# The product with w_out by seven quarter products, its weight sums split early and kept in DRAM

## The chip, the cores and the metric

The kernel runs on one core of a Trainium2 chip. The metric is the time of one execution on the device in microseconds (us), the median of three runs. A difference of 0.2% is 2.4 us here.

The engines are named as in the profile: PE multiplies matrices (PEld is its weight load), DVE, ACT and POOL work elementwise, SP issues the DMAs between DRAM and the on-chip memory. Each runs its own instructions in order.

## The reference

It is one block of a streaming encoder, for 1024 tokens of width 1024 and 16 meta tokens ahead of them. What matters here:

```python
z = einsum('bld,dn->bln', rmsnorm(h), w_in)          # a, q, k, v, r, lr, ga, gb
p = pool_mix(multiscale_pool(a)) * pool_scale        # four groups of 128 channels
y_a = p @ w_pool_out
y_b = (rmsnorm(gla(q, k, v, log_a)) * silu(r)) @ w_gla_out
m = sigmoid(ga) * y_a + sigmoid(gb) * y_b
h = h + m @ w_out                                    # the product that is changed
h = h + square(relu(rmsnorm(h) @ w_ff1)) @ w_ff2
return rmsnorm(h)[:, N_META:]
```

## The kernel before

**Products.** All is float32. A factor is kept as two fp32r parts, high and low (`w1h`, `w1l`; `th`, `tl`), and `mm3` (L281 to L287) multiplies by three matmuls: high by high (L285), and the two mixed ones (L286, L287). One matmul is 128x128 by 128x512 at most. To split a factor, ACT copies its high part and DVE subtracts that for the low part. PE runs its matmuls in the order of the program text; for DVE, ACT, POOL and SP a scheduler sets an order when the kernel is built.

**The stage of the a-blocks** (60 to 150 us). After the value projections come four blocks `a_block(g)` (PE, 72 matmuls of two 264-column pieces and one of 512 columns for each of the three parts), the decays, and `mix_block(g)`: DVE makes the trailing sums `s` of group g (L665, one to four instructions of 128 x 1024 or a little more), subtracts the token (L668), ACT and DVE split the outcome into `ph` (L671, L672), and PE multiplies it by a 128x128 matrix, six matmuls to the banks `b_mm` and `b_sc`. The list in the text is a0, decays 0, a1, decays 1, mix 0, a2, mix 1, a3, mix 2, k0, mix 3; then come `differences`, which takes the differences of the input's quarters (`xr`) and splits them to `t0`, `t1`, `t2` (ACT L704, DVE L705), and k1. The weights of each block are loaded by SP to two buffers `raw`. From 150 us on POOL makes sums of weights for the later products (`fs`, `s`, L810).

**The merge stage** (480 to 590 us). The blocks `yb(j)` for the second half of the tokens multiply by w_gla_out, and DVE joins the outcome with `gb` and `ma`, which SP loads from DRAM to lent buffers `o` and `t` (L1137, L1195, L1196); the outcome is split to `MH`, `ML`. `load_wo` loads w_out in 256-row pieces by 512 columns and splits it in place. `out_tile(t, ch)` is the product with w_out for 128 tokens and 512 output columns: 8 contraction blocks of 3 matmuls, in all 8 x 2 x 24 = 384 matmuls of 128x512. Its outcome is added to the input x in `acc`, followed by the layer norm, a store of h, and `turn_tile`, which transposes the rows for the feed-forward product and makes the quarter differences for it. Three `mm` banks and three `ms` banks are there.

Of the kernel before, what the change touches and what calls it, by code (L numbers as in the profile page):

```python
# [7 lines left out]
F32 = mybir.dt.float32  # L8
# [6 lines left out]
P = 128  # L15
# [107 lines left out]
def kernel(  # L123
# [55 lines left out]
    h_dram = dp.tile([8, P, D], F32, name="h_dram")  # L179
    hf_dram = [dp.tile([NPAIR, P, HALF], F32, name=f"hf{m}_dram") for m in range(7)]  # L180
# [425 lines left out]
    def decays(p):  # L606
        def fn():
            for half, c in enumerate(halves()):
                y = nxt("c")
                log_decay(S["lr"][:, c], p, HALF, y, nxt("t1"))  # L610
                act.activation(y, y, ACT.Exp, scale=1.0 / TAU)
                nc.sync.dma_start(decay_dram[p, half], y)
                yield 0.6
            if p:
                act.activation(gnorm, gnorm, ACT.Copy, scale=0.5)
            log_decay(S["lr"][:, SEQ : SEQ + META], p, META, metab[:, META_LOG[p]], metab[:, 4])
            if p:
                tc.keep_in_program_order(act.preload_act_table_set("exp_and_others"))

        return fn  # L620

    def pool_open():
# [4 lines left out]
        lr_turn()  # L627
        act.activation(S["gu"], wgu, ACT.Copy)
# [62 lines left out]

    def differences():

        left.pop_to(S["left_t"])
# [25 lines left out]
    for f, i in ((a_, 0), (d_, 0), (a_, 1), (d_, 1), (m_, 0), (a_, 2), (m_, 1), (a_, 3), (m_, 2), (k_, 0), (m_, 3)):  # L720
        f(i)
# [365 lines left out]
    def gla_open():  # L1087
        left.pop_to(S["left_t"])
        right.pop_to(0)
        S["yg"] = {h: right.push(f"yg{h}", [P, 2, HEADS, HALF], F32R) for h in (1, 0)}  # L1090
# [81 lines left out]
    def yb_block(j, h):  # L1172
        def fn(wb=None):
# [8 lines left out]
            for e in range(2):  # L1182
                d, w = 2 * j + e, slice(e * P, (e + 1) * P)
                ask()
                gl, ml = take("b", d, h)
                b = bank("mm")
# [8 lines left out]
                dve.scalar_tensor_tensor(gl, gl, 1.0, b, ALU.add, ALU.mult)  # L1195
                dve.tensor_tensor(gl, gl, ml, ALU.add)  # L1196
                th = MH[h][:, d]
                tl = ML[h][:, d]
                act.activation(th, gl, ACT.Copy, scale=0.5)
                dve.scalar_tensor_tensor(tl, gl, 0.5, f32(th), ALU.mult, ALU.subtract)  # L1200
# [111 lines left out]

    def merge_open():
        banks(keep=2, ms=3)
        left.pop_to(left_m)
        right.pop_to(1)
        S["wo"] = [left.push("wo0", [P, 2, KT, HALF], F32R)]
# [3 lines left out]
        S["left2"] = left.mark()  # L1321
        buffer("t1", 4)
        buffer("o", 4)
        lend("t1", "o")
        wanted[:] = [("b", 2 * j + e, 1) for j in MERGE for e in range(2)]
        ask()
        raw.lend(left.push("raw3", [P, D], F32))
        nc.sync.dma_start(gB, bcast(norm_ffn))

    def x_again(*rows):  # L1330
        for t in rows:
            tc.keep_in_program_order(nc.sync.dma_start(S["acc"][:, t], x[t * P : (t + 1) * P, :]))

    def load_wo(ch, kk):
        def fn():
            wo = S["wo"][ch][:, :, 2 * kk : 2 * kk + 2]
            c = slice(ch * HALF, (ch + 1) * HALF)
            src = w_out[kk * 256 : (kk + 1) * 256, c].rearrange("(k p) c -> p k c", p=P)
            if ch:
                r = raw.load(src, D).rearrange("p (k c) -> p k c", k=2)  # L1340
            else:
                r = S["acc"][:, 4 + kk].rearrange("p (k c) -> p k c", k=2)
                nc.sync.dma_start(r, src)
            act.activation(wo[:, 0], r, ACT.Copy)
            dve.tensor_tensor(wo[:, 1], r, f32(wo[:, 0]), ALU.subtract)

        return fn

    step(rest, merge_open)
    def wo1_open():  # L1350
        raw.back()
        left.pop_to(S["left2"])
        right.pop_to(0)
        S["u2p"] = right.push("u2p", [P, 2, HALF], F32)
        raw.lend(right.push("rawx0", [P, D], F32))
        S["right_ff"] = right.mark()
        S["wo"].append(right.push("wo1", [P, 2, KT, HALF], F32R))


    ORDER = (0, 4, 1, 5, 2, 3, 6, 7)  # L1360

    def out_tile(t, ch):
        def fn():
            half, at = t // 4, (t % 4) * P
            wo = S["wo"][ch]
            if ch == 0 and t < 6:
                x_again(t + 2)
            if ch == 0 and t == 6:
                act.activation(gB, gB, ACT.Copy, scale=-0.5)
            b, n = bank("mm"), ORDER.index(t)  # L1370
            for j in range(2):
                if ch and j and n > 1:
                    turn_tile(ORDER[n - 2])
# [4 lines left out]
            a = S["acc"][:, t, ch * HALF : (ch + 1) * HALF]  # L1378
            dve.tensor_tensor(a, b, a, ALU.add)
            if ch:  # L1380
                layer_norm(S["acc"][:, t], S["u2"][:, n % 2])
                nc.sync.dma_start(h_dram[t], S["acc"][:, t])

        return fn

    def turn_tile(t, tags=("ms",)):
# [3 lines left out]
        u, acc, g = S["u2"][:, ORDER.index(t) % 2], S["acc"], t % 4  # L1390
# [21 lines left out]
        dve.tensor_tensor(hi, hi, lo, ALU.subtract)  # L1412
        for n, a in enumerate((lo, b12)):
            fh, fl = (S["wo"][0][:, k, 4 * n : 4 * n + 4, cols] for k in range(2))
            act.activation(fh, a, ACT.Copy)
            dve.tensor_tensor(fl, a, f32(fh), ALU.subtract)
# [4 lines left out]
    yb(2)  # L1421
    for k in range(4):
        step(rest, load_wo(0, k))
    yb(3)
    yb(0)
    step(rest, lambda: x_again(0, 1))
    step(rest, out_tile(0, 0))
    yb(1)
    step(rest, out_tile(1, 0))
    step(rest, wo1_open)  # L1430
    for t in range(2, 8):
        step(rest, out_tile(t, 0))
        if t < 6:
            step(rest, load_wo(1, t - 2))


# [3 lines left out]
    def first_blocks():  # L1440
        raw.n = 0
        for i, u in ((0, 0), (0, 1), (1, 0)):
            load_ff(i, u)

    step(rest, first_blocks)
    for t in ORDER[:6]:
        step(rest, out_tile(t, 1))
    step(rest, lambda: ff_weights())
    for t in ORDER[6:]:
        step(rest, out_tile(t, 1))  # L1450

    def ff_weights():
# [4 lines left out]
        n = lambda j: tuple(S["wo"][0][:, k, 4 * j : 4 * j + 4] for k in range(2))  # L1457
        S["x"] = {"P1": m(0, 0), "P2": m(0, 1), "P5": m(1, 0), "P3": m(1, 1), "P6": n(0), "P7": n(1)}

    def ff_open():  # L1460

        right.pop_to(S["right_ff"])
        S["fs"] = right.push("fs", [P, 2, HALF], F32)
        S["s3"] = right.push("s3", [P, HALF], F32)
        S["u3p"] = right.push("u3p", [P, 2, HALF], F32)
        S["x"]["P4"] = tuple(right.push("t4" + k, [P, 4, HALF], F32R) for k in "hl")
        raw.lend(right.push("rawx1", [P, D], F32))
        load_ff(1, 1)

    def ff_room():  # L1470

        fh, fl = S["x"]["P4"]
# [207 lines left out]
    def ff_layers():  # L1680
# [3 lines left out]
        for n in range(4):  # L1684
            if n in (1, 3):
                turn_tile(ORDER[6 + n // 2], ("mm", "ms"))
            next(run)
# [51 lines left out]
```

## Time and profile before

| | us |
|---|---|
| median of 3 runs (lowest, highest) | 1210.67 (1210.05, 1210.98) |
| span of the profiled execution | 1209.1 |
| between that span and the median | 1.6 |
| PE busy in the span | 1194.4 (99%) |
| DVE busy | 837.5 (69%) |
| ACT busy | 574.4 (48%) |
| POOL busy | 79.1 (7%) |

The profile shows one execution; the runs' times hold besides the span what the program needs to start and to end. A page row with a line, an engine and "out<-in" stands for a group of instructions by the program's names. A row of the timeline has the start in us, the busy time in us, the engine, the line, the operation with shapes, how many instructions it stands for, and in brackets the idle time before and what ended it. In the rows of the 40 slices each digit is the busy share of 30.2 us in tenths.

### The profile page before, as it was taken

The numbers are of one execution on the slowest core, as the hardware profiler recorded it, in microseconds if no ns is written. First come the engines' busy times: TensorE is split into PE (matmuls) and PEld (weight loads), VectorE is DVE, ScalarE is ACT, GpSimd is POOL, SyncE is SP. The second block draws the span as 40 slices with busy tenths as digits, with TensorE's granted clock in tenths as the row PEclk, the third lists the DMA queues.
The fourth block names the chain that finished last, engine by engine and source line by source line (L and its number), as shares of the span: only waits on it lengthen the run. The fifth ranks groups of instructions, "written<-read, shape, count | busy, mean of one in ns | idle before, by whom it ended". The sixth has DMA issues, their size and how long they took to land.

```text
span 1209.1 us, 18303 instructions
## 1 busy us (share of the span) xinstructions
PE 1194.4 (99%) x6775; PEld 993.1 (82%) x6775; DVE 837.5 (69%) x1369; ACT 574.4 (48%) x1014; POOL 79.1 (7%) x97
## 2 busy tenths in 40 slices
PE   9999999999999999999999999999999999999997
PEld 7999877878778887788788888888888888888886
DVE  6636567565686669726887767677675887887686
ACT  7546444444456124305655545455464444444554
POOL 0000062323320000000000000000000000000000
PEclk9999999999999999999999999999999999999999
DMA  8223253534348978812255444444479963333532
GB/s 245 77 60 123 91 133 110 166 110 146 112 138 296 315 218 268 284 32 87 88 161 168 151 139 157 148 160 151 152 253 318 348 229 98 98 100 91 173 96 88
DMA packets 151385, 192.79 MB, mean 159 GB/s; under 512 B 12216, under 2 KB 86256, under 8 KB 151296
## 3 DMA queue, kind: packets, MB, share of 16 engines
q1 hardware_dynamic: 151136, 191.56, 49.5%
q8 instruction: 53, 0.87, 0.3%
q14 instruction: 36, 0.29, 0.1%
q10 hardware_dynamic: 160, 0.07, 0.0%
HBM read 128.66 MB, written 62.93 MB: 158 GB/s over the span
## 4 chain that ended last, share of the span: by engine, by line
PE 68%; DVE 3%; issue 1%; DMA 1%; ACT 1%; DVEq 0%; ACTq 0%
PE b_oa L287 5%; PE b_oa L285 5%; PE b_oa L286 5%; PE b_y L285 4%; PE b_y L286 4%; PE b_y L287 4%; PE b_mm L285 4%; PE b_mm L287 4%; PE b_mm L286 4%; PE b_ob L287 4%; PE b_ob L285 4%; PE b_ob L286 4%; PE b_z L286 3%; PE b_z L285 3%; PE b_z L287 3%; PE b_sc L285 2%
## 5 line engine op out<-in xcount | busy, mean ns | idle before, releaser
L774 ACT ACTIVATE w1h<-raw 128x512 fp32r<-128x512 f32 x106 | 65.8, 622 | 51.2 <-PE b_sc L286 21.2
L285 PE MATMUL b_sc<-th,w1h 128*128 128x512 f32 x216 | 85.4, 395 | 0.4 <-ACT u2p L1522 0.4
L285 PE MATMUL b_z<-th,w1h 128*128 128x512 f32 x216 | 84.9, 393 | 0.4 <-DVE c L893 0.4
L775 DVE TENSOR_TENSOR w1l<-raw,w1h 128x512 fp32r<-128x512 f32 x106 | 72.5, 685 | 18.0 <-ACT w1h L774 18.0
L286 PE MATMUL b_sc<-tl,w1h 128*128 128x512 f32 x216 | 84.8, 393 | 0.0
L286 PE MATMUL b_z<-tl,w1h 128*128 128x512 f32 x216 | 84.2, 390 | 0.4 <-DVE tl L1408 0.4
L287 PE MATMUL b_sc<-th,w1l 128*128 128x512 f32 x216 | 84.4, 391 | 0.0
L287 PE MATMUL b_z<-th,w1l 128*128 128x512 f32 x216 | 84.1, 389 | 0.0
L774 ACT ACTIVATE w1h<-fs 128x512 fp32r<-128x512 f32 x81 | 51.1, 630 | 67.0 <-PE b_y L286 33.6
L775 DVE TENSOR_TENSOR w1l<-fs,w1h 128x512 fp32r<-128x512 f32 x81 | 57.7, 712 | 23.7 <-ACT w1h L774 23.7
L285 PE MATMUL b_mm<-th,w1h 128*128 128x512 f32 (+1 forms) x208 | 72.0, 346 | 0.0
L287 PE MATMUL b_mm<-th,w1l 128*128 128x512 f32 (+1 forms) x208 | 71.1, 342 | 0.0
L286 PE MATMUL b_mm<-tl,w1h 128*128 128x512 f32 (+1 forms) x208 | 71.0, 342 | 0.0
L774 ACT ACTIVATE w1h<-bt 128x512 fp32r<-128x512 f32 x46 | 29.1, 632 | 70.8 <-issue 43.9
L1598 DVE TENSOR_TENSOR bt<-w,w 128x512 f32<-128x512 f32 x80 | 54.7, 683 | 2.7 <-DMA w<-in_w_ff_dram 2.7
L285 PE MATMUL b_mm<-wo,th 128*128 128x512 f32 x128 | 50.4, 394 | 0.9 <-PE b_mm L287 0.9
L287 PE MATMUL b_mm<-wo,tl 128*128 128x512 f32 x128 | 49.9, 390 | 0.0
L286 PE MATMUL b_mm<-wo,th 128*128 128x512 f32 x128 | 49.8, 389 | 0.0
L285 PE MATMUL b_y<-wo,w1h 128*128 128x512 f32 x128 | 49.8, 389 | 0.0
L286 PE MATMUL b_y<-wo,w1h 128*128 128x512 f32 x128 | 49.8, 389 | 0.0
L287 PE MATMUL b_y<-wo,w1l 128*128 128x512 f32 x128 | 49.8, 389 | 0.0
L775 DVE TENSOR_TENSOR w1l<-bt,w1h 128x512 fp32r<-128x512 f32 x46 | 31.8, 691 | 25.6 <-ACT w1h L774 25.6
(425 smaller groups left out, 3317.1 us busy)
## 6 DMA issues: line engine op xcount, KB each, us to landing
hf_dram<-h SPq DMA_DIRECT2D x112, 256.0 KB, 2.1
raw<-hf_dram SPq DMA_DIRECT2D x112, 256.0 KB, 2.6
w<-in_w_ff_dram SPq DMA_DIRECT2D x64, 256.0 KB, 4.8
raw<-in_w_in_dram SPq DMA_DIRECT2D x22, 512.0 KB, 4.7
raw<-in_w_ff_dram SPq DMA_DIRECT2D x16, 512.0 KB, 4.1
rawx<-in_w_ff_dram SPq DMA_DIRECT2D x16, 512.0 KB, 4.1
rawp<-in_w_in_dram SPq DMA_DIRECT2D x10, 512.0 KB, 4.2
xs<-in_x_dram SPq DMA_DIRECT2D x8, 512.0 KB, 4.8
```

The costliest lines, as they stand in the source:

```text
L285: pe.matmul(ps, ah, bh, start=first and i == 0, stop=False, skip_group_check=more)
L286: pe.matmul(ps, ah, bl, start=False, stop=False, skip_group_check=more)
L287: pe.matmul(ps, al, bh, start=False, stop=last and i == n - 1, skip_group_check=more)
L774: act.activation(hi, a, ACT.Copy)
L775: dve.tensor_tensor(lo, a, f32(hi), ALU.subtract)
L1598: dve.tensor_tensor(bt, w, S["w2"][q[3:]][:, i], ALU.add if q[2] == "+" else ALU.subtract)
```

## The change

The product with w_out is done by seven products of quarters (the form of Strassen's method that reuses sums) in place of the eight that its four quarters would need: `product(p, t)` for p in P1 to P7 and four token tiles of 128, each 4 contraction blocks of 3 matmuls, in all 7 x 4 x 12 = 336 matmuls of 128x512. Four of the seven weights are sums of w_out's quarters (T1 to T4).

These sums are made in the stage of the a-blocks, in four parts k of 128 rows each. A part loads four 256 KB pieces of w_out to `wr`; POOL makes four differences in two 256-column instructions each (L712 of the new file); ACT copies the high part of each to `ws` (L713); POOL subtracts it for the low part (L715), again in two instructions; SP writes high and low to the new `ws_dram` (L717). That makes 64 instructions of POOL, 16 of ACT and 48 DMAs in the four parts. `wr` holds one part, `ws` two differences. `wr` and `ws` lie at the end of the on-chip memory where `differences` later puts the top of `t2`, so it begins with `right.pop_to(3)`.

In the merge stage the second half's outcomes stay unsplit in `acc`, those of the first half are written to `mo_dram` and read again; `first_sums` and `last_sums` make the token sums on DVE, ACT and POOL; `ready` reads the finished weight sums from `ws_dram`, `staged` loads and splits the plain quarters. The blocks `yb` have four halves of `u2` as their buffers for `gb` and `ma`; two `mm`, two `x` and two `ms` banks are there. PE adds P6, P7 and P4 to banks that hold earlier products, and ACT, POOL and DVE add the banks to x in `acc`. The gates' factor 0.5 is taken into earlier scales.

```diff
+        S["wr"] = right.push("wr", [P, 4, HALF], F32)
+        S["ws"] = right.push("ws", [P, 2, 2, HALF], F32R)
...
+    def wo_load(k):
+        for j in range(4):
+            nc.sync.dma_start(S["wr"][:, j], wo_rows(j, k))
+
+    def wo_sums(k):
+
+        b11, b12, b21, b22 = (S["wr"][:, j] for j in range(4))
+        both = (slice(0, 256), slice(256, HALF))
+        for n, (to, a, b) in enumerate(((b11, b12, b11), (b12, b22, b12), (b22, b22, b11), (b21, b21, b22))):
+            hi, lo = (S["ws"][:, n % 2, u] for u in range(2))
+            for c in both:
+                pool.tensor_tensor(to[:, c], a[:, c], b[:, c], ALU.subtract)
+            act.activation(hi, to, ACT.Copy)
+            for c in both:
+                pool.tensor_tensor(lo[:, c], to[:, c], f32(hi[:, c]), ALU.subtract)
+            for u, a in enumerate((hi, lo)):
+                nc.sync.dma_start(ws_dram[(0, 2, 1, 3)[n], k, u], f32(a))
...
     def differences():
 
+        right.pop_to(3)
         left.pop_to(S["left_t"])
...
-    for f, i in ((a_, 0), (d_, 0), (a_, 1), (d_, 1), (m_, 0), (a_, 2), (m_, 1), (a_, 3), (m_, 2), (k_, 0), (m_, 3)):
+    o_ = lambda k: step(one, wo_ahead(k))
+    step(one, lambda: wo_load(0))
+    for f, i in (
+        (a_, 0), (o_, 0), (d_, 0), (a_, 1), (o_, 1), (d_, 1), (m_, 0), (a_, 2), (o_, 2), (m_, 1), (a_, 3), (o_, 3), (m_, 2),
+        (k_, 0), (m_, 3),
+    ):
...
     def merge_open():
-        banks(keep=2, ms=3)
+        banks(keep=1, mm=2, x=2, ms=2)
...
+        buffer("u2", 2, D)
+        S["io"] = [S["u2"][:, i, c] for i in range(2) for c in halves()]
...
-    def out_tile(t, ch):
...
-                mm3(
-                    b, KT // 2, lambda i: (MH[half][:, 4 * j + i, at : at + P], ML[half][:, 4 * j + i, at : at + P]),
-                    lambda i: (wo[:, 0, 4 * j + i], wo[:, 1, 4 * j + i]), first=j == 0, last=j == 1,
-                )
...
+    def product(p, t):
...
+        mm3(b, 4, lambda k: (ah[:, k, c], al[:, k, c]), lambda k: (w[:, 0, k], w[:, 1, k]), first=first, more=not first)
+        (c11, c12), (c21, c22) = ([S["acc"][:, 4 * r + t, h] for h in halves()] for r in range(2))
+        if p in ("P1", "P6", "P7"):
+            act.activation(c21, b, ACT.Copy)
+            pool_add({"P1": c11, "P6": c12, "P7": c22}[p], c21)
+            return
```

Lines of the new file are numbered anew: L665, L668, L672 and L705 of before are L670, L673, L677 and L741, and L1137 is L1179.

**DVE, from the first mix block's sums on.** The names: `s` the trailing sums of a mix block, `ph` its split factor, `metab` small values of the meta tokens, `t2l` the low part of the last difference, `xr` the input. Before, `t2l` stands ahead of all the mix blocks:

```order
L400 COPY lrtok<-b_mm 16x16
L705 TENSOR_TENSOR t2l<-xr,t2h 128x2048
L412 TENSOR_TENSOR lr<-b_ms,lr 16x16
L412 TENSOR_TENSOR lr<-b_ms,lr 16x512 x2
L85 TENSOR_TENSOR w1l<-raw_120,w1h 128x1024
L665 TENSOR_TENSOR s<-a 128x1024
L668 SCALAR_TENSOR_TENSOR s<-s,a 128x1024
```

Now it stands between the sums and the subtraction of the last mix block, g = 3 (the four L670 are that block's sums):

```order
L670 TENSOR_TENSOR s<-a 128x1038
L670 TENSOR_TENSOR s<-s 128x1036
L670 TENSOR_TENSOR s<-s 128x1032
L670 TENSOR_TENSOR s<-s 128x1024
L741 TENSOR_TENSOR t2l<-xr,t2h 128x2048
L673 SCALAR_TENSOR_TENSOR s<-s,a 128x1024
L677 TENSOR_TENSOR ph<-s,ph 128x512 x2
```

`t2l` has moved behind some forty rows, and since its memory was that of `wr` and `ws`, it has gained waits: for POOL's last instruction of the sums and for the last writes to `ws_dram`. L673 and the `ph` of mix 3 stand behind it.

**ACT, at the second mix block.** `a` is the evacuation of an a-block, `ph` the split factor of mix 1, `c` the evacuation of a mix product. Before:

```order
L677 ACTIVATE c<-b_sc,small 128x512
L652 ACTIVATE a<-b_mm 128x264 x2
L671 ACTIVATE ph<-s 128x512 x2
L84 ACTIVATE w1h<-raw_120 128x1024
L652 ACTIVATE a<-b_mm 128x512
```

Now:

```order
L657 ACTIVATE a<-b_mm 128x264
L713 ACTIVATE ws<-wr 128x512 x2
L676 ACTIVATE ph<-s 128x512 x2
L84 ACTIVATE w1h<-raw_122 128x1024
L657 ACTIVATE a<-b_mm 128x512
L713 ACTIVATE ws<-wr 128x512
```

Two copies of part 2 (of 0 to 3), each of which waits for differences that POOL makes, stand ahead of mix 1's `ph`; copies of part 1 stand in the same way ahead of mix 0's.

**SP, at the block yb(3) of the merge stage.** Before, the pairs of `gb` and `ma` follow each other with a load of w_out now and then:

```order
L1137 DMA o<-gb_dram 128x512
L1137 DMA o<-ma_dram 128x512
L1137 DMA o<-gb_dram 128x512
L1137 DMA o<-ma_dram 128x512
L1343 DMA acc<-in_w_out_dram 128x2x512
L1137 DMA t_4683<-gb_dram 128x512
```

Now four loads of x, and elsewhere four of w_out, stand between two pairs:

```order
L1398 DMA tmp<-in_w_out_dram 128x512 x2
L1243 DMA mo_dram<-o 128x512
L1388 DMA acc<-in_x_dram 128x512 x4
L1179 DMA u_4826<-gb_dram 128x512
L1179 DMA u_4826<-ma_dram 128x512
L1179 DMA u_4826<-gb_dram 128x512
L1179 DMA u_4826<-ma_dram 128x512
L1398 DMA tmp<-in_w_out_dram 128x512 x4
```

The pairs go to four buffers in place of the eight of `t` and `o`, and stand behind the loads of the staged quarters.

More of the change, by code (lines that the diff above doesn't have):

```diff
@@ L1328, in merge_open @@
+        S["tmp"] = right.push("tmp", [P, 4, HALF], F32)
+        staged("P1")
         nc.sync.dma_start(gB, bcast(norm_ffn))
[L1330 to L1347, printed above, removed]
```

248 lines of the change are left out of this document (174 added, 74 removed).

## The prediction

> **What bounds the kernel now.** The page comes first: its busy times, then its 40 slices.
>
> ```profile
> span 1209.1 us, 18303 instructions
> PE 1194.4 (99%) x6775; PEld 993.1 (82%) x6775; DVE 837.5 (69%) x1369; ACT 574.4 (48%) x1014; POOL 79.1 (7%) x97
> PE   9999999999999999999999999999999999999997
> POOL 0000062323320000000000000000000000000000
> PEclk9999999999999999999999999999999999999999
> ```
>
> PE is at work in every slice at full clock; POOL works only from the sixth slice (151 us) to the twelfth. So time is saved only by taking matmuls away, and lost wherever PE is made to wait. The waits of PE today are small, by its longest ones:
>
> ```profile
> PE b_ms L474 <- POOL xr L459: 1.5, 1, 1.5
> PE b_gs L995 <- DVE gi L1050: 1.0, 2, 0.7
> PE b_mm L285 <- DVE o L1195: 0.9, 1, 0.9
> ```
>
> (Total, times, longest.) After a start-up wait of 1.5 us none is over 1.0 us. PE's order is that of the text, so a wait on any block's operands holds back all that follows.
>
> **The matmuls that go.** In the product with w_out the timeline of PE shows
>
> ```profile
> 501.11 0.39 PE L285 MATMUL b_mm<-wo,th 128*128 128x512 f32 x1
> 502.47 0.39 PE L285 MATMUL b_mm<-wo,th 128*128 128x512 f32 x1
> ```
>
> Between these lie six matmuls: 1.36 / 6 = 0.2267 us each. 384 become 336, so 48 x 0.2267 = **10.9 us** of PE goes. That is the whole gain; DVE and ACT work that goes or comes is worth nothing by itself.
>
> **What is added early.** The sums for four of the weights are made while PE runs the a-blocks. POOL is idle there today; the price is in its groups (busy, mean ns, idle before) and in two pairs of 128x256 instructions:
>
> ```profile
> L810 POOL TENSOR_TENSOR s<-rawp,rawp 128x256 f32<-128x256 f32 x10 | 7.2, 739 | 15.3 <-DVE w1l L775 15.3
> L810 POOL TENSOR_TENSOR fs<-raw,fs 128x256 f32<-128x256 f32 x12 | 11.7, 994 | 20.3 <-DVE w1l L775 17.4 <-DVE small L1045 2.9
> 152.92 1.43 POOL L810 TENSOR_TENSOR s<-raw,raw 128x256 f32<-128x256 f32 x2
> 224.75 2.40 POOL L810 TENSOR_TENSOR fs<-fs,raw 128x256 f32<-128x256 f32 x2 [3.73 <-DVE w1l L775]
> ```
>
> The first pair took 1.43 us, 0.715 each; the second, the same work, 2.40 us. What ran beside the second on DVE:
>
> ```profile
> 224.59 0.83 DVE L1019 TENSOR_TENSOR f<-gi,g 128x512 f32<-128x512 f32 x1
> 225.32 1.22 DVE L1030 TENSOR_TENSOR n<-n,g 128x512 f32<-128x512 f32 x1
> L1030 DVE TENSOR_TENSOR n<-n,g x4: 679/702/1220, 169.9 to 337.1; 128x512 f32<-128x512 f32 x4
> ```
>
> The DVE instruction took 1.22 us against 0.68 at best (minimum, median, maximum stand in the last row): from 225.32 it waited for POOL's first, then POOL's second waited for it. Both read two operands from on-chip memory. So POOL loses about one DVE instruction's length whenever such a one runs beside it.
>
> Now the chain of the four parts. SP issues part 0's loads just ahead of a weight load; the costs of the transfers are on the page (us to landing).
>
> ```profile
> 71.32 17.13 SPq L118 DMA_DIRECT2D raw<-in_w_in_dram  x2
> 472.63 0.45 SPq L1137 DMA_DIRECT2D o<-gb_dram  x1
> hf_dram<-h SPq DMA_DIRECT2D x112, 256.0 KB, 2.1
> raw<-hf_dram SPq DMA_DIRECT2D x112, 256.0 KB, 2.6
> w<-in_w_ff_dram SPq DMA_DIRECT2D x64, 256.0 KB, 4.8
> ```
>
> First loads landed: 71.3 + 2.6 = 73.9. Four parts of 16 POOL instructions: 4 x 16 x 0.715 = 45.8 us. Between two parts the next part's second load waits on SP behind the last write of this one: 2 x 0.45 + 2.6 = 3.5 us, three times 10.5. So POOL ends at 130.2 us if nothing hinders it. DVE has this to do until then:
>
> ```profile
> core 0: us, PE busy (x) PEld busy (x) DVE busy (x) ACT busy (x) POOL busy (x), PEclk, DMA share, GB/s
> 100.00:137.00 37.00, 37.00 (x230) 33.53 (x229) 25.42 (x33) 20.83 (x39) 0.00 (x0) 1.00 0.39 121
> 75.16 2.29 DVE L705 TENSOR_TENSOR t2l<-xr,t2h 128x2048 fp32r<-128x2048 f32 x1 [1.78 <-ACT t2h L704]
> 127.15 3.76 DVE L665 TENSOR_TENSOR s<-s 128x1036 f32<-128x1036 f32 x3
> 130.95 1.22 DVE L668 SCALAR_TENSOR_TENSOR s<-s,a 128x1024 f32<-128x1024 f32 x1
> 132.93 1.29 DVE L672 TENSOR_TENSOR ph<-s,ph 128x512 fp32r<-128x512 f32 x2 [0.76 <-ACT ph L671]
> 134.14 0.17 DVE L966 TENSOR_TENSOR metab<-metab 128x16 f32<-128x16 f32 x1
> 135.26 2.29 DVE L705 TENSOR_TENSOR t0l<-xr,t0h 128x2048 fp32r<-128x2048 f32 x1 [0.95 <-ACT t0h L704]
> 136.36 0.39 PE L285 MATMUL b_mm<-ph,mw 128*128 128x512 f32 x1
> ```
>
> Of 25.4 us DVE busy from 100 to 137, some 4.4 belong to 130.95 and after (1.22 + 1.29 + 0.17 + the 1.74 of a 2.29 us split that begins at 135.26); 21.0 us run before, nearly all with both operands on chip. POOL is at work in 45.8 / 56.3 = 0.81 of its chain, so 0.81 x 21.0 = **17.0 us** is what it loses. The bounds are 0 (DVE falls into POOL's gaps, or doesn't hinder it) and 21.0 plus some 3 for what runs from 74 to 100, so 24. I take 17, since the two pairs above show a full exchange turn by turn. POOL ends at 147.2.
>
> **Who waits for POOL.** In the new order `t2l`, which ran at 75.16, stands on DVE between the sums and the subtraction of mix 3, and it waits for POOL's last instruction and the last write. Behind it stand L668's successor, the `ph` of mix 3 and all that DVE does later. So: POOL's end + issue and landing 0.45 + 2.1 + `t2l` 2.29 = +4.8; then from L668's start to the first `ph` pair's end, 130.95 to 132.93 + 0.65, 2.6 us. Mix 3's second matmul, which reads the low `ph`, can run at POOL's end + 7.4; PE wants it at 136.36 + 0.23 = 136.6. Unhindered: 130.2 + 7.4 - 136.6 = 1.0 us lost. With 17.0 us of hindrance: **18.0 us**; at the upper bound 25. Today the same `ph` is ready at 133.6, 3.0 us ahead of PE. That cover is gone, and PE has nothing else to run.
>
> The ACT copies that wait for POOL stand ahead of mix 0's and mix 1's `ph` too; what PE waits there counts within the 18, since it shifts PE's wish for mix 3 by as much. Nothing makes this good later: the products after mix 3 need DVE and PE alike, and PE is at full load.
>
> That PE sits idle for many us in one piece is not seen in this trace. [...]
>
> The other early edits cost nothing. 48 transfers of 256 KB, 12 MB, are added where the DMA share is 0.39 in the windows row above. The weight loads of the later blocks wait on SP behind the writes that POOL releases; PE is late by as much, so they stay ahead of it.
>
> **The merge stage.** It is the other place of PE's small waits.
>
> ```profile
> 480.00:500.00 20.00, 18.33 (x80) 14.89 (x81) 15.71 (x24) 5.66 (x8) 0.00 (x0) 1.00 0.93 314
> 520.00:540.00 20.00, 20.00 (x90) 16.57 (x89) 3.98 (x6) 0.96 (x2) 0.00 (x0) 1.00 0.00 1
> 480.80 0.50 PE L285 MATMUL b_mm<-yg,w1h 128*128 128x512 f32 x1 [0.90 <-DVE o L1195]
> 490.12 0.47 PE L285 MATMUL b_mm<-wo,th 128*128 128x512 f32 x1 [0.87 <-PE b_mm L287]
> 482.26 0.69 DVE L1195 SCALAR_TENSOR_TENSOR t<-t,b_mm 128x512 f32<-128x512 f32 x1 [1.51 <-DMA t<-gb_dram]
> ```
>
> Around 480 to 500 us the DMAs are 0.93 busy, DVE waits for `gb` and PE for DVE. From 520 to 540 DVE is busy 3.98 of 20 us and the DMAs are idle: the new token sums (28 DVE instructions of 0.69) and the reads of the finished weights (32 of 256 KB) fit there. In `yb`, one pair of buffers serves every second block: a slot comes free 1.3 us (two DVE instructions) after the block before last, then two issues 0.9 and a landing of 2.6 to 4.8, in all 4.8 to 7.0 against the two blocks of 24 x 0.2267 = 5.4 us. At 4.8 nothing is lost and the two waits of today, 1.8 us, go; at 7.0, with four such turns in the eight blocks, 6.4 us are lost less 1.8. I take +1.0, since the landing of `gb` today at 0.93 share was late by 1.51, and keep -1.8 and +4.6.
>
> **The sum.** -10.9 + 18.0 + 1.0 = +8.1. The span goes from 1209.1 to 1217.2; with the 1.6 us that lie around it 1218.8, the same as 1210.67 + 8.1.
>
> **Rivals.**
> - *POOL is little hindered.* DVE works in bursts and partly in POOL's gaps; the loss is 1 to 7 us, so 1210.7 - 10.9 + 1 + 1 = 1201.8 up to 1207.8: faster. For it: most POOL pairs in the page's groups mean well under 0.9 us each, since DVE is busy 0.69 of the span and yet doesn't always meet them. Against it: POOL's chain fills 0.81 of the stretch, not 0.07 as over the span now. [...]
> - *A middle case*: some 8 to 12 us lost to POOL's chain, 1208.8 to 1212.8: no change. For it: half of the 21.0 us of DVE work hindering, 0.5 x 21.0 + 1.0 = 11.5.
> - [...]
> - *The merge stage loses its pace too*: two `mm` banks and four buffers, loads at 4.8 us or more behind four loads of x: +4.6 in place of +1.0, so 1222.4; it decides from landings of over 4 us on.
>
> **How the numbers follow.** Chances: the likeliest 0.40 (its own range 1214 to 1223, from 13 to 22 us of loss), the clock case 0.10, the merge case 0.08, together 0.58 slower; little hindered 0.29 faster; the middle 0.13 the same. What 0.2% means is 2.4 us, so "same" is 1208.3 to 1213.1. The range takes in the middle and nearly all of the little-hindered case, and the clock and merge cases: 1202 to 1224. Outside it lie the case of two late mechanisms at once and the upper bound of 25 us lost.
>
> **What would show it right or wrong.** In the changed profile PE has one long wait, or some, at the mix blocks around 115 to 160 us, ended by DVE's or ACT's `ph`, 13 to 22 us in all, and the timeline of DVE shows `t2l` there after a long idle stretch, released by POOL or a DMA. POOL's pairs between 74 and 147 us take 1.43 to 2.4 us, in all over 55 us for the 64 instructions. From mix 3 to the first `yb` of the second half the two traces run in step. Between the last `yb` and the first feed-forward product 10 to 11 us go. It is wrong if PE waits less than 8 us in the stage of the a-blocks, or if POOL's 64 instructions take under 50 us; then the time is below 1209. It is wrong in the other way if PE waits over 5 us within the seven products.

## The result, and the profile after

The changed kernel takes 1249.55 us (median of 4 runs, 1246.54 to 1251.36) against 1210.61 for the kernel before beside it: a ratio of 1.032 (95% interval 1.0305 to 1.0334), 38.9 us slower. Forecast were 1218.8 us and a range up to 1224. (One of the four runs of f_all, further down, took 1697.9 us at a mean granted clock of 0.65, where its other three had 0.99; it is not counted there.) The page of the changed kernel, its busy times and slices:

```profile
span 1244.8 us, 18681 instructions
PE 1198.3 (96%) x6727; PEld 991.6 (80%) x6727; DVE 869.2 (70%) x1385; ACT 593.4 (48%) x1059; POOL 186.5 (15%) x217
PE   9997799999999999889889999999999999999997
POOL 0048533333221000361320000000000000000000
PEclk9998989999999999899999999999999999999999
```

Two balances can be read from it. PE has 48 matmuls less and should be busy for 1194.4 - 10.9 = 1183.5 us; it is busy for 1198.3, so 14.8 us were lost while it worked. Its idle time went from 1209.1 - 1194.4 = 14.7 to 1244.8 - 1198.3 = 46.5 us, 31.8 more. 31.8 + 14.8 - 10.9 = 35.7, the difference of the two spans. The three slices with an 8 in the row of PE's clock (a slice is 31.1 us here) lie in two places: among and just behind the a-blocks (the 4th and the 6th) and in the merge stage (the 17th; further short stretches stay within a 9). The windows (columns as before: stretch, then length, busy times by engine, granted clock, DMA share) show the slow stretches:

```profile
116.00:126.00 10.00, 6.78 (x33) 6.21 (x33) 9.86 (x9) 4.04 (x8) 9.64 (x9) 0.66 0.59 199
150.00:162.00 12.00, 6.53 (x23) 5.63 (x24) 7.88 (x7) 7.00 (x8) 0.00 (x0) 0.57 0.76 241
506.00:514.00 8.00, 6.77 (x17) 5.33 (x18) 3.95 (x7) 2.94 (x5) 1.45 (x3) 0.57 1.01 379
556.00:562.00 6.00, 5.70 (x18) 4.50 (x19) 1.37 (x2) 0.84 (x2) 3.98 (x5) 0.72 0.66 210
622.00:626.00 4.00, 3.69 (x14) 3.23 (x15) 3.76 (x8) 2.87 (x9) 0.00 (x0) 0.58 0.32 131
```

PE's busy time times what the clock lacks: 6.78 x 0.34 + 6.53 x 0.43 + 6.77 x 0.43 + 5.70 x 0.28 + 3.69 x 0.42 = 11.2 of the 14.8 us. Ahead of each stretch stands a wait of PE (3.23, 7.41, 3.62, 3.42 and 2.26 us). PE's waits by what ended them, the longest sums:

```profile
PE b_mm L287 <- ACT ph L676: 8.3, 2, 7.4
PE b_mm L287 <- DVE acc L1240: 5.4, 2, 3.6
PE b_sc L287 <- ACT acc L1438: 4.8, 3, 3.4
PE b_mm L288 <- DVE ph L677: 4.5, 2, 3.2
PE b_ms L1493 <- DVE u L261: 2.3, 1, 2.3
```

The two rows of `ph` are the mix blocks, the other three the merge stage. How late PE is after the first stage, the same pair product in both traces says; first before, then after:

```profile
174.43 0.50 PE L285 MATMUL b_z<-th,w1h 128*128 128x512 f32 x1 [0.37 <-DVE c L893]
```

```profile
196.87 0.50 PE L287 MATMUL b_z<-th,w1h 128*128 128x512 f32 x1 [0.43 <-DVE c L934]
```

22.4 us are lost by then. From there on the two traces run in step up to the merge stage (22.2 us apart at 460.69 of the first trace), and again from the first feed-forward products to the end (35.6 apart at 649.27 and at 899.29). So the rest of the 35.7, 13.3 us, is lost between the second half's `yb` and the first feed-forward products, in short the merge stage, which had 10.9 to save: it loses 24.2.

From the last transposes ahead of these `yb` to the first product that reads `t4l` (columns as in the windows above), before, after, and in e1_no_early and m8_turn_late, two runs further down:

```profile
461.46:613.65 152.19, 149.44 (x686) 122.69 (x685) 104.07 (x166) 64.05 (x115) 0.00 (x0) 1.00 0.43 146
483.61:649.48 165.87, 147.20 (x638) 117.52 (x637) 118.67 (x181) 74.65 (x143) 53.38 (x56) 0.96 0.59 199
461.41:629.89 168.48, 147.78 (x638) 117.89 (x637) 118.94 (x182) 74.77 (x143) 53.44 (x56) 0.95 0.59 201
460.14:616.16 156.02, 143.06 (x638) 114.03 (x637) 119.99 (x185) 75.55 (x143) 43.84 (x48) 0.99 0.62 212
```

PE's idle time here is the length less its busy time: 2.8 us before, 18.7 after. With 15.9 us of new waits and about 6 of slow clock (147.20 x 0.04) some 22 of the 24 us are found.

**Among the a-blocks**, DVE and POOL in the changed kernel:

```profile
94.67 0.66 DVE L998 TENSOR_TENSOR metab<-metab 128x8 f32<-128x8 f32 x1
142.11 5.02 DVE L670 TENSOR_TENSOR s<-s 128x1036 f32<-128x1036 f32 x3
151.33 2.29 DVE L741 TENSOR_TENSOR t2l<-xr,t2h 128x2048 fp32r<-128x2048 f32 x1 [4.21 <-DMA ws_dram<-ws]
```

```profile
L715 POOL TENSOR_TENSOR ws<-wr,ws 128x256 fp32r<-128x256 f32 x32 | 32.4, 1041 | 3.6 <-ACT ws L713 1.8 <-DMA ws_dram<-ws 1.7
L712 POOL TENSOR_TENSOR wr<-wr 128x256 f32<-128x256 f32 x32 | 23.6, 766 | 19.1 <-DMA wr<-in_w_out_dram 19.1
```

```profile
140.94 8.15 POOL L715 TENSOR_TENSOR ws<-wr,ws 128x256 fp32r<-128x256 f32 x6
```

A DVE instruction of 128x8 elements takes 0.66 us where it took 0.17 (at 95.56 us of the trace before), 0.49 longer, which is less than one POOL instruction of 0.715; the three sums of mix 3 take 5.02 instead of 3.76; POOL's instructions have means of 766 and 1041 ns instead of 715. POOL's last instruction ends at 149.1, the write lands at 151.3, `t2l` runs, then mix 3's subtraction, and the last to wait is PE, for 7.4 us, and then at half speed:

```profile
155.47 0.80 PE L287 MATMUL b_mm<-ph,mw 128*128 128x512 f32 x1 [7.41 <-ACT ph L676]
156.79 0.63 PE L289 MATMUL b_mm<-ph,mw 128*128 128x512 f32 x1
157.22 0.63 PE L287 MATMUL b_sc<-ph,mw 128*128 128x512 f32 x1
```

From 156.79 to 157.22 are 0.43 us, a little less than twice 0.2267.

**In the merge stage**, PE's three largest waits, with what follows at once in the text below:

```profile
507.23 0.79 PE L287 MATMUL b_mm<-fo,w1h 128*128 128x512 f32 x1 [3.62 <-DVE acc L1240]
...
556.30 0.50 PE L287 MATMUL b_sc<-wo,fo 128*128 128x512 f32 x1 [3.42 <-ACT acc L1438]
...
622.31 0.80 PE L1493 MATMUL b_ms<-ident,u 128*128 128x128 f32 x4 [2.26 <-DVE u L261]
```

The first is in `yb(3)`. SP's queue ahead of it:

```profile
496.52 0.33 SPq L1243 DMA_DIRECT2D mo_dram<-o  x1
499.50 1.75 SPq L1388 DMA_DIRECT2D acc<-in_x_dram  x4
501.30 0.43 SPq L1179 DMA_DIRECT2D u<-gb_dram  x1
```

The loads of x wait until the last write out of `o` has landed, since `acc` takes that memory over, and `gb` for `yb(3)` stands behind them. On DVE, though, the instruction that ended PE's wait stood idle for only 0.47 us because of `gb`; until then DVE was at work on two splits of weights that stand ahead of it:

```profile
502.37 2.49 DVE L1402 TENSOR_TENSOR wo<-tmp,wo 128x512 fp32r<-128x512 f32 x4
504.79 1.22 DVE L85 TENSOR_TENSOR w1l<-raw,w1h 128x1024 fp32r<-128x1024 f32 x1
506.49 0.69 DVE L1240 SCALAR_TENSOR_TENSOR acc<-u,b_mm 128x512 f32<-128x512 f32 x1 [0.47 <-DMA u<-gb_dram]
```

So the late `gb` is the last of several causes of this wait and by itself a small one. The second is P6's second token tile, which takes the other half of the `sc` pair while the first half is not yet evacuated. ACT, before it evacuates it (L1438):

```profile
555.13 0.63 ACT L1455 ACTIVATE th<-acc 128x512 fp32r<-128x512 f32 x1 [3.48 <-DVE acc L1475]
555.67 0.58 ACT L1438 ACTIVATE acc<-b_sc 128x512 f32<-128x512 f32 x1
```

ACT stood for 3.5 us in front of a split of the token sums, with the evacuation behind it. The third is the layer norm of the tile that P4 finishes late.

### The profile page after: what moved, and what is told of

It reads as the page before. It is cut to its first block, busy times and chain, and to the rows that moved or that the text cites. A ratio compares the mean times of both kernels' runs of the same rounds, so it can differ in the third digit from the quotient of the medians.

```text
span 1244.8 us, 18681 instructions
## 1 busy us (share of the span) xinstructions
PE 1198.3 (96%) x6727; PEld 991.6 (80%) x6727; DVE 869.2 (70%) x1385; ACT 593.4 (48%) x1059; POOL 186.5 (15%) x217
## 5 line engine op out<-in xcount | busy, mean ns | idle before, releaser
L815 ACT ACTIVATE w1h<-raw 128x512 fp32r<-128x512 f32 x114 | 70.8, 623 | 74.3 <-PE b_sc L288 35.3
L816 DVE TENSOR_TENSOR w1l<-raw,w1h 128x512 fp32r<-128x512 f32 x114 | 78.2, 687 | 37.2 <-ACT w1h L815 37.2
L287 PE MATMUL b_y<-fo,w1h 128*128 128x512 f32 x128 | 49.9, 390 | 1.7 <-ACT w1h L815 1.7
L289 PE MATMUL b_y<-fo,w1l 128*128 128x512 f32 x128 | 49.9, 390 | 0.1
L287 PEld LDWEIGHTS b_sc<-th,w1h 128*128 128x128 f32 x216 | 40.9, 189 | 11.5 <-ACT u2p L1655 1.8
L288 PE MATMUL b_y<-fo,w1h 128*128 128x512 f32 x128 | 49.8, 389 | 0.0
L816 DVE TENSOR_TENSOR w1l<-bt,w1h 128x512 fp32r<-128x512 f32 x46 | 31.8, 691 | 25.6 <-ACT w1h L815 25.6
L287 PEld LDWEIGHTS b_z<-th,w1h 128*128 128x128 f32 x216 | 40.5, 188 | 9.7 <-DVE c L934 0.9
L289 PEld LDWEIGHTS b_sc<-th,w1l 128*128 128x128 f32 x216 | 40.9, 189 | 9.0
```

Of the source, the lines that this page charges most:

```text
L287: pe.matmul(ps, ah, bh, start=first and i == 0, stop=False, skip_group_check=more)
L288: pe.matmul(ps, ah, bl, start=False, stop=False, skip_group_check=more)
L289: pe.matmul(ps, al, bh, start=False, stop=last and i == n - 1, skip_group_check=more)
L815: act.activation(hi, a, ACT.Copy)
L816: dve.tensor_tensor(lo, a, f32(hi), ALU.subtract)
```

## The experiments

All times are medians beside runs of the kernel before on the same chip, 1209.5 to 1209.8 us. Behind each stands its ratio to the kernel before, with the 95% interval in brackets; it is not taken from the two medians and can differ a little from their quotient.

### The first stage and the merge stage apart

**e1_no_early** takes the early sums out:

```diff
-    step(one, lambda: wo_load(0))
-        (a_, 0), (o_, 0), (d_, 0), (a_, 1), (o_, 1), (d_, 1), (m_, 0), (a_, 2), (o_, 2), (m_, 1), (a_, 3), (o_, 3), (m_, 2),
-        (k_, 0), (m_, 3),
+        (a_, 0), (d_, 0), (a_, 1), (d_, 1), (m_, 0), (a_, 2), (m_, 1), (a_, 3), (m_, 2), (k_, 0), (m_, 3), (o_, 0),
...
+            for u in range(2):
+                nc.sync.dma_start(ws_dram[0, 0, u], f32(S["ph"][:, u, :HALF]))
```

> The changed kernel without the early sums: no w_out loads, POOL differences, copies or writes among the a-blocks; the merge stage reads as many bytes of finished weights, but all from one place that two writes after mix 3 fill, so the weight sums are left out and the product is another. The two traces put 22.4 us of lateness at the first pair product behind the a-blocks (196.87 against 174.43) and 35.7 at the end. Theory, two separate losses: the first goes whole, the second stays: 1249.6 - 22.4 = 1227, 1225 to 1229. Rival, the merge stage is late because of what the early part left behind (its writes to DRAM, its SP queue): then the time comes below 1222.

1220.3 us, 1.0098 [1.0066, 1.013]. That is below 1222, on the rival's side. **e2_early_only** puts the same sums alone into the kernel before:

> The kernel before with the early sums alone, whose outcome nobody reads. Theory: the loss among the a-blocks is the whole 22.4 us that the two traces show: 1210.6 + 22.4 = 1233, 1231 to 1235, with t2l as the last gate before mix 3. Rival, part of that loss is made by other parts of the change (the scales, the place of buffers): below 1228.

1236.5 us, 1.0214 [1.0197, 1.0232]. Both missed their intervals and the sum held: +10.6 and +26.8 are 37.4, against 38.9 for the whole change. So the losses are separate, nearly all of it: the early sums cost 26.8 us without any change in the merge stage, which leaves the rival of e1 some 1.5 us (38.9 - 37.4), less than these runs scatter. The early part costs 27 to 29 us, more than the 22.4 of the one pair of traces. The profiled run of e1 took 1226.9, its other three 1218 to 1222; one trace is one draw of a time that now scatters, and e1's is its slowest.

### What holds PE among the a-blocks

**e3_t2_late** holds `t2l`'s subtraction in the order of the text:

```diff
-            dve.tensor_tensor(lo, a, f32(hi), ALU.subtract)
+            i = dve.tensor_tensor(lo, a, f32(hi), ALU.subtract)
+            if p == "P4":
+                tc.keep_in_program_order(i)
```

> The changed kernel with t2l held in the order of the text on DVE, so that mix 3's subtraction and ph no longer stand behind it; POOL's chain stays as long. Theory: mix 3 then waits for the sums s alone, which end at 147.1; ph at about 149.7 and not 155.5, so the wait of 7.4 us falls to 1 to 2 and the slow clock behind it (3.3 us) goes: 1249.6 - 9 = 1240.5, 1239 to 1243. Rival, ACT's copies or the later blocks hold PE as long: 1247 or more.

1247.0 us, 1.0299 [1.0266, 1.0332]: at the edge of what the rival gives, and not clear of no gain. The theory that `t2l` is the one gate fell. ACT and PE in this run:

```profile
142.65 0.63 ACT L713 ACTIVATE ws<-wr 128x512 fp32r<-128x512 f32 x1 [2.87 <-POOL wr L712]
143.19 1.04 ACT L84 ACTIVATE w1h<-raw 128x1024 fp32r<-128x1024 f32 x1
144.13 0.58 ACT L657 ACTIVATE a<-b_mm 128x512 f32<-128x512 f32 x1
```

```profile
144.76 0.59 PE L287 MATMUL b_mm<-th,w1h 128*128 128x264 f32 x1 [7.21 <-ACT a L657]
```

The evacuation of a3 stands on ACT behind two copies of part 3, which wait for POOL; PE waits for the bank. **e8_o3_late** takes both gates away; with them all of part 3, its loads and POOL's work too, moves behind mix 3 in the text:

```diff
-        (a_, 0), (o_, 0), (d_, 0), (a_, 1), (o_, 1), (d_, 1), (m_, 0), (a_, 2), (o_, 2), (m_, 1), (a_, 3), (o_, 3), (m_, 2),
-        (k_, 0), (m_, 3),
+        (a_, 0), (o_, 0), (d_, 0), (a_, 1), (o_, 1), (d_, 1), (m_, 0), (a_, 2), (o_, 2), (m_, 1), (a_, 3), (m_, 2),
+        (k_, 0), (m_, 3), (o_, 3),
...
-            act.activation(hi, to, ACT.Copy)
+            i = act.activation(hi, to, ACT.Copy)
+            if k == 3:
+                tc.keep_in_program_order(i)
...
-        parts("P4", b21)
-        S["last_difference"] = lambda: parts("P5", b11)
+        S["last_difference"] = lambda: (parts("P4", b21), parts("P5", b11))
```

> The changed kernel with part 3 of the sums put behind mix 3 in the text, its four ACT copies held in that order, and t2l held behind the last difference's other parts. The run with t2l alone held late gained nothing clear: there PE waited 7.2 us for the evacuation of a3, which stood on ACT behind two copies of part 3. Theory, two gates in a row on POOL's chain, t2l on DVE and the copies on ACT: with both out of the way the waits of 7.4 and 0.9 us and the slow clock of some 3.3 us behind them go, those before mix 1 stay, and up to 4 us come back where t2l now stands ahead of the first pair's weights: 1249.6 - 11.6 + 0 to 4 = 1238 to 1242. Rival, whatever comes next behind POOL's chain waits as long, since it is the chain's length that PE has to sit out: 1246 or more.

1236.7 us, 1.0218 [1.0182, 1.0254], 12.8 less than the changed kernel and 1.3 below the interval of the theory. PE no longer waits at mix 3 (the trace is of the fastest of four runs, 1230.2 us). Its longest wait in this stage is now the one for `t2l`:

```profile
162.65 0.50 PE L288 MATMUL b_y<-t2l,w1h 128*128 128x512 f32 x1 [2.69 <-DVE t2l L743]
```

`t2l` runs at 160.31 on DVE, straight behind two other splits and 3.1 us after POOL's last instruction; the trace shows no wait of DVE for POOL there. What the ACT copies cost alone, with `t2l` left where it was, no run shows.

**e4_half_pool** leaves out POOL's and ACT's work for two of the four differences, and leaves every transfer:

```diff
+            if n < 2:
                 for c in both:
                     pool.tensor_tensor(to[:, c], a[:, c], b[:, c], ALU.subtract)
                 act.activation(hi, to, ACT.Copy)
...
```

> The changed kernel with POOL's and ACT's work for two of the four differences of each part left out, and all 48 transfers kept (the third and fourth write the first two's values, so half of the weight sums are wrong). Theory, POOL's length is the cause: its chain ends some 20 us earlier, mix 3 does not wait, and of the 22.4 us only the first waits remain: 1249.6 - 18 = 1231, 1228 to 1235. Rival, the transfers and the SP queue are the cause: 1243 or more.

1230.4 us, 1.0172 [1.0156, 1.0187], 19.2 less. The transfers alone are not it: with all of them in place POOL's chain ends at 130.2 us, and PE's wait at mix 3 is 1.1. POOL's work and the ACT copies that follow it went together here, so their shares stay open. **e9_memset** asks whether POOL and DVE hinder each other by reading:

```diff
-                pool.tensor_tensor(to[:, c], a[:, c], b[:, c], ALU.subtract)
+                pool.memset(to[:, c], 0.0)
+                pool.memset(to[:, c], 1.0)
...
-                pool.tensor_tensor(lo[:, c], to[:, c], f32(hi[:, c]), ALU.subtract)
+                pool.memset(f32(lo[:, c]), 0.0)
+                pool.memset(f32(lo[:, c]), 1.0)
```

> The changed kernel with each of POOL's differences and low parts replaced by two memsets of the same 128x256 piece, which write and read nothing; copies, transfers and waits stay, the weight sums are left out. In the changed profile the small DVE instructions on metab take 0.65 to 0.72 us where they took 0.17, and POOL's pairs 1.43 to 3 us. Theory, POOL's reads and DVE's second operand exclude each other: without reads the small ones take 0.17 again, 128x1024 sums 1.2 and not 1.7, POOL's chain is short, and the time falls to that of the kernel without early sums and a few us of copies: 1220 to 1230. Rival, POOL hinders DVE by any access, or DVE is slowed by the transfers: the small ones stay over 0.4.

1227.1 us, 1.0148 [1.0135, 1.0161]. DVE's small instructions, beside POOL's memsets:

```profile
95.99 0.17 DVE L999 TENSOR_TENSOR metab<-metab 128x8 f32<-128x8 f32 x1
96.19 0.17 DVE L1000 TENSOR_TENSOR metab<-metab 128x8 f32<-128x8 f32 x1
```

```profile
94.87 0.56 POOL L712 MEMSET wr<- 128x256 f32 x2 [1.81 <-DMA wr<-in_w_out_dram]
95.89 0.56 POOL L716 MEMSET ws<- 128x256 f32 x2
```

With POOL at work from 95.9 to 97 us they take 0.17 again. The memsets are also shorter, 0.28 each, which shortens POOL's chain too, so the time of the run tells little here, and the rows tell it: 0.59 to 0.72 with POOL's reads, 0.16 to 0.17 beside its writes alone, nothing between (sixteen such instructions in each trace, those of the second not all beside POOL). Whether the second operand of the DVE instruction takes part, as the theory has it, no run shows.

### What a wait costs

**c1_wait5** and **c2_wait8** put one wait into the kernel before:

```diff
             pp = nxt("s")
+            if g == 3:
+                for _ in range(5):
+                    dve.tensor_tensor(pp[:, :SEQ], cur[:, META:e], a[:, META:e], ALU.add)
```

> The kernel before with one PE wait put in: five more DVE instructions of 128x1024 (their outcome is overwritten) ahead of mix 3's subtraction, nothing else. DVE is 5 x 1.15 + 0.6 later with ph (one split of weights falls in between), 3.0 us of cover stand against it, so PE waits some 3.1 us once. Theory, a wait costs itself and a stretch at half clock behind it: 3.1 + 2.5 = 5.6, 1215.3. Rival, a wait costs itself alone: 1212.6.

> The same with eight such instructions: PE waits some 6.6 us once. Theory: 6.6 + 2.5 to 3.4 = 9 to 10, 1219. Rival, itself alone: 1216.1.

1215.9 us, 1.005 [1.0036, 1.0064], and 1219.1 us, 1.0079 [1.0066, 1.0091]: +6.0 and +9.3. The wait of the first and the window behind it, then those of the second:

```profile
140.03 0.49 PE L285 MATMUL b_mm<-ph,mw 128*128 128x512 f32 x1 [3.14 <-ACT ph L674]
140.76 0.79 PE L286 MATMUL b_mm<-ph,mw 128*128 128x512 f32 x1 [0.23 <-DVE ph L675]
```

```profile
140.00:145.00 5.00, 4.74 (x19) 3.95 (x20) 3.58 (x3) 4.53 (x5) 0.00 (x0) 0.66 0.16 61
```

```profile
143.04 0.79 PE L285 MATMUL b_mm<-ph,mw 128*128 128x512 f32 x1 [6.92 <-ACT ph L674]
```

```profile
143.00:148.50 5.50, 5.46 (x20) 4.54 (x21) 3.59 (x3) 5.03 (x5) 0.00 (x0) 0.57 0.25 93
```

Waits of 3.4 and 6.9 us cost 6.0 and 9.3 by the medians: each some 2.5 more than itself. By the traces it is less: PE is 5.4 and 8.4 us late right behind (the product at 137.84 us before starts at 143.28 and 146.28), 2.1 and 1.5 more than the waits. The windows show 4.74 x 0.34 = 1.6 and 5.46 x 0.43 = 2.3 us as slow clock. The rival, itself alone, is out.

The length of a wait does not settle whether the clock falls. Over all the traces of this case, PE has 18 waits of 3.4 us or more behind the first 20 us (3.42, 3.62 and 7.41 in the changed kernel, 7.21 in e3_t2_late and 6.92 in c2_wait8 are among them), and within 2.5 us after each the granted clock falls to a half. Of 62 waits from 1.59 to 3.31 us, 33 have it; of 30 from 1.0 to 1.55 none. The same wait for the same layer norm has it in the changed kernel (2.26 us, the last row of the slow stretches above) and not in e1_no_early, where PE waits 2.28 us until 600.80:

```profile
600.80:604.80 4.00, 4.00 (x22) 3.46 (x23) 3.93 (x9) 3.33 (x9) 0.00 (x0) 1.00 0.32 131
```

So a wait of 1.6 to 3.3 us is priced by a chance and not by a fixed sum.

### Where the merge stage loses

All of these start from e1_no_early, 1220.3. **m5_x_late** moves the x loads behind `yb(3)`:

```diff
-        for t in range(4):
-            x_quarter(0, 0, t)
...
     yb(3)
+    later(lambda: [x_quarter(0, 0, t) for t in range(4)])
```

> The kernel without the early sums, with the four loads of x for the first quarter moved behind yb(3). In its trace PE waits 3.9 us in yb for DVE, which waits for gb; gb's load stands on SP behind the x loads, and these wait for the last write of mo_dram out of the buffers that acc takes over. Theory: that wait and the slow clock behind it go, some 5 us: 1220.3 - 5 = 1215, 1213 to 1217. Rival, two mm banks and four buffers hold the pace whatever stands on SP: 1219 or more.

1220.2 us, 1.0093 [1.0076, 1.0109]: no gain by the medians, though the wait shrank from 3.9 to 1.6 us in the traces.

```profile
482.87 0.50 PE L287 MATMUL b_mm<-fo,w1h 128*128 128x512 f32 x1 [1.62 <-DVE acc L1237]
```

**m6_sc_alt** lets P1's tiles take `sc` and `x` banks in turn:

```diff
-            b = in_x[t] = bank("sc" if t < 2 else "x")
+            b = in_x[t] = bank("x" if t % 2 else "sc")
```

> The kernel without the early sums, with P1's tiles on sc and x banks in turn (sc, x, sc, x) in place of sc, sc, x, x. PE waits 0.7, 3.4 and 0.7 us for ACT's evacuation of the tile before, each time at the second tile on the sc pair, which is one buffer of two banks. Theory, the second half of the pair waits for the first half's evacuation: with another bank in between these 4.9 us go, 1220.3 - 4.9 = 1215.4, 1213 to 1217. Rival, ACT's evacuation of P6 is late anyway and the wait moves to the third tile: 1219 or more.

1222.5 us, 1.0104 [1.0089, 1.0119]: no gain. The three waits on `sc` are gone from the trace, and others have grown: 2.66 us ahead of P2 (2.01 in e1) and 2.21 at 545.59.

```profile
514.28 0.50 PE L287 MATMUL b_mm<-wo,th 128*128 128x512 f32 x1 [2.66 <-DVE acc L1237]
```

**m9_no_sums** leaves out the token sums (`first_sums`, and in `last_sums` all but the loads):

> The kernel without the early sums, also without the token sums of the merge stage (first_sums and the sums and splits of last_sums are left out; products P1, P6, P2 and P5 take what lies in those places). Matmuls and weight transfers stay. Theory, the waits ahead of P2 (2.0 us) and P6 (3.4) come from DVE and ACT queues in which the sums and their splits stand ahead of the evacuations: they go, with a slow clock of 2 to 3 us: 1220.3 - 8 = 1212, 1209 to 1215. Rival, banks, buffers and transfers set the pace: 1218 or more.

1217.7 us, 1.007 [1.0056, 1.0085], between the two: 2.6 us less than e1, where the theory had 8. In its trace the wait ahead of P2 is gone and that of P6 is down from 3.4 to 0.8, as the theory has it, and the one in `yb(3)` is 4.1. The wait ahead of P2 does come from the sums: it is 1.8 us or more in every trace that keeps them. That of P6 is less sure, since it is 1.2 in m5's trace with the sums in place. Either way the sums are a small part of the time.

**m10_no_ready** leaves out three quarters of the reads of the finished weights:

> The kernel without the early sums, with 24 of the 32 reads of finished weights in the merge stage left out (three of four blocks of P6's, P5's, P7's and P4's weights keep what lay there). Theory, the reads are not what PE waits for, nor what delays gb: 1218 to 1222. Rival, the DMA share of 0.86 to 0.96 in this stage is the cause of the late transfers: below 1214.

1223.9 us, 1.012 [1.0102, 1.0138]: above the interval, and no gain, so these reads are not the cause. **m7_three** joins m5 and m6 and gives DVE the quarter difference of `turn_tile` back; **m8_turn_late** adds to these the last two transposes one step later:

```diff
-        for c in (slice(0, 2), slice(2, 4)):
-            pool.tensor_tensor(hi[:, c], hi[:, c], lo[:, c], ALU.subtract)
+        dve.tensor_tensor(hi, hi, lo, ALU.subtract)
...
-            if n in (1, 3):
-                turn_tile(6 + n // 2, ("mm", "ms"))
+            if n in (2, 3):
+                turn_tile(4 + n, ("mm", "ms"))
```

> Both of these, and the quarter difference of turn_tile on DVE again and not on POOL; ACT's split of it stands ahead of the evacuation for which PE waits 3.0 us at the start of the feed-forward products. Theory, the waits add up: 1220.3 - 5 - 4.9 - 3 = 1207.4, 1204 to 1211, about the kernel before. Rival, DVE becomes the gate of the stage and each wait only moves: 1214 or more.

> The kernel without the early sums, with the x loads late, sc and x banks in turn, the quarter difference on DVE, and in addition the last two turn_tile calls one step later among the feed-forward products (before the third and fourth, in place of the second and fourth). Theory, the last layer norms end too late for the transposes because P4's last tiles come last: with 2.7 us more for them the waits of 0.9 and 0.4 us go, and 1217.1 becomes 1214 to 1216. Rival, the wait moves to the product that reads the turned tokens: 1217 or more.

1217.1 us, 1.0053 [1.0037, 1.0069], and 1214.5 us, 1.0044 [1.0028, 1.0059]. The first missed its interval, the second met it. Four moves together bring 5.8 us by the medians, while the waits that they went for had 14.0 in e1's trace (3.9 + 0.7 + 3.4 + 0.7 + 3.0 + 2.3). In the windows of the merge stage above, PE's idle time falls from 168.48 - 147.78 = 20.7 us in e1 to 156.02 - 143.06 = 13.0 in m8: 7.7 of the 14.0, and the rest turned up at other places. The two lengths differ by 12.5 us, more than the medians, because e1's trace is of its slowest run and holds more slow clock (0.95 against 0.99). The rival that m5 and m6 name, two banks and four buffers that set the pace, has no run of its own. **f_all** is the complete change with all the moves of both stages:

> The changed kernel, complete, with all the single moves that took a wait away: part 3's copies and t2l late, x loads late, sc and x banks in turn, the quarter difference on DVE, the last turn_tile calls one step later. Theory, the gains of the two stages add: 1249.6 - 12.8 - 5.8 = 1231, 1227 to 1235. Rival, the waits of one stage decide alone: 1240 or more. Below the kernel before it does not come by either.

1229.8 us (three runs, 1229.6 to 1231.0), 1.0169 [1.0153, 1.0184], 19.7 less than the changed kernel and 20.0 over the one before: the gains of the two stages, 12.8 and 5.8, add. No version here beats the kernel before.

## Why the prediction was wrong, point by point

In the profiled run the span was to be 1217.2 us and was 1244.8. Of these 27.6 us, 24.2 - 1.0 = 23.2 are the merge stage's and 22.4 - 18.0 = 4.4 the first stage's. The step that failed is the term of the merge stage.

- *The matmuls that go, -10.9.* Right: 48 fewer on the page, at 0.2267 us.
- *POOL's chain, its end at 147.2.* It ended at 149.1, by two errors that cancel, so that the near hit is luck. POOL lost 56.0 - 45.8 = 10.2 us to DVE and not 17.0. Its waits within the chain took about 20 us and not 10.5: some 16 for the loads of the next parts (the 19.1 of the page less 3.2 ahead of and within the first part), the rest for ACT's copies, for writes out of `ws` and within the first part. The loads landed after 3.6 us (median of the page) and not 2.6, and stood on SP behind the writes of more than one difference, the last ones behind `pm_dram` writes as well. That POOL and DVE lengthen each other while POOL reads was right (DVE's 128x8 instructions take 0.59 to 0.72 us beside POOL's differences and 0.17 beside the memsets of e9_memset; POOL's means are 766 and 1041 ns in place of 715), and that the chain's length counts (e4_half_pool, 19.2 us less).
- *The wait at mix 3, 18.0.* Mix 3 came at 155.47 against 136.36, 19.1 late, and DVE's `t2l` stood there as forecast. That `t2l` is what holds it was half the truth: ACT's copies of part 3 hold PE as long by a second way (e3_t2_late), and the two had to go together (e8_o3_late). The ACT copies were named for mix 0 and mix 1 alone. That the sum came within 1.1 us of the 19.1 is luck too, as the end of POOL's chain is; 2.3 us of the 19.1 are slow clock (116 to 126 us), which the sum left out.
- *The slow clock left out of the sum.* Here the prediction failed by its own choice: its sum has no term for a slow clock, and the clock case, a slow clock behind the long wait, has a chance of 0.10. That case was the author's estimate, and the trace before does not show it: behind the first 20 us none of PE's waits there is over 1.0 us, and the granted clock is 1.00 until PE's work ends. What the runs showed in its place: one wait with a slow clock behind it costs 1.5 to 2.6 us beyond itself (c1_wait5, c2_wait8), and the changed kernel has five, 11 of the 14.8 us. Behind mix 3 it brings the lateness of the first stage from 19.1 to 22.4. Over all the traces it follows 18 of 18 waits of 3.4 us or more, but also 33 of 62 from 1.59 to 3.31 us.
- *The merge stage, +1.0 with bounds -1.8 and +4.6.* This is the step that failed: it was 24.2 in the trace, 10.6 + 10.9 = 21.5 by e1_no_early. Only `yb`'s buffers were priced there, and all else was put at nothing. That DVE was busy for 3.98 of 20 us between 520 and 540 was taken for proof that the sums are hidden; but P2 and P6 wait for them, and the evacuations that free banks stand behind them on ACT and DVE (m9_no_sums; that alone is 2.6 us of the time). Within the seven products PE waits 1.8 + 4.8 + 0.7 = 7.3 us, over the 5 us that the prediction named as the sign of being wrong this way. The end of the stage, the last layer norms, evacuations and splits behind P4, was not priced at all: 2.3, 1.6 and 1.7 us in three waits.
- *The rivals.* The clock case and the merge case came together, and the merge case at about five times its price of 4.6; both were held to be exclusive. The range left just that out.

What stays open: which part of the merge stage would have to change for its waits to vanish and not to move. Four moves of single instructions gave 5.8 of the 21.5 us, leaving the token sums out 2.6. More buffers for `gb` and `ma` and a third `mm` bank were not tried, and the cause of most of this loss is not shown.

## What to carry to other kernels

Where one engine is at 99%, every instruction that is new on a queue from which that engine is fed has to be priced at the place where it stands in order, and by all the queues that wait for the same slow chain; taking one gate away shows the next. A count of idle time in a window says only that work fits, not that nobody waits for it. And a stall of PE can cost more than its length: 6.0 us for a wait of 3.4 in c1_wait5, 9.3 for one of 6.9 in c2_wait8.

## What the runs showed of the hardware

- A single PE wait of 3.4 or 6.9 us costs 1.5 to 2.6 us more than itself; the granted clock is at a half for 3.4 and 4.7 us behind it (c1_wait5, c2_wait8).
- Over all traces the granted clock falls to a half behind 18 of 18 waits of PE of 3.4 us or more, 33 of 62 from 1.59 to 3.31 us, and none of 30 from 1.0 to 1.55. The stretch lasts 2.9 to 6.4 us, most often 3.4 (in the changed kernel 6.4 behind the wait of 7.41, 3.4 behind those of 3.42 and 2.26).
- DVE instructions of 128x8 elements with two on-chip operands take 0.59 to 0.72 us in place of 0.17 while POOL runs differences of 128x256 (the changed kernel against the one before), and 0.17 beside POOL's memsets (e9_memset).
- Kernels with several waits of PE scatter more: 8.7 us over four runs of e1_no_early and 10.1 over four of e8_o3_late, against up to 2.4 over nine of the kernel before on one chip. It is not so with each: c1_wait5 and c2_wait8, with one wait each, scatter by 1.5 and 1.1 over five, m9_no_sums by 1.2 over four. The mean granted clock of a run takes part in it (0.992 in e1's run of 1226.9 us, 0.995 in its two of 1218), by an estimate some 4 of the 8.7 us (0.003 x 1220); the rest is open.
